# Last block of a streaming encoder step: weight sums behind the pooled frames, pooled products behind za, quarters laid out one by one

## The chip, the cores and the metric

The kernel runs on one core of a Trainium2 chip. The metric is the device time of one execution in microseconds (us). The core has five engines that each work through their own list of instructions in order: TensorE (PE in the profile, with the weight loads as PEld) for matrix products, VectorE (DVE), ScalarE (ACT), GpSimd (POOL) and SyncE (SP). SP does no arithmetic here; its list is a queue of DMA issues. An engine that waits for a semaphore holds everything behind that instruction in its list.

## The reference

One layer of an encoder trunk over 2048 prompt frames and 32 sample frames of width 1024, cut to what the change touches:

```python
hn = rmsnorm(h, g_mix)
hA, bA, cA, zA, vB, zB = split(hn @ w_in)          # six projections of width 512 each
u  = cA * hA
c  = uu[0:T]*conv_w[0] + uu[1:1+T]*conv_w[1] + uu[2:2+T]*conv_w[2] + conv_b   # uu: history, then u
yA = bA * c * silu(zA)
for g, w in enumerate((2, 4, 8, 16)):              # four groups of 128 channels
    pooled_g = trailing_mean(vB_g, w) - vB_g
yB = (pooled @ pool_w) * pool_scale * silu(zB)
h  = h + concat(yA, yB) @ w_out
h  = h + (p @ w_ple) * sigmoid(rmsnorm(h, g_ple) @ w_ple_gate)
y  = rmsnorm(h, g_final)
```

The last two frames of u and the last 15 of vB are returned as well, as states of the streams.

## The kernel before

**Precision.** A product in full float32 accuracy is made of three matmuls on a high and a low part. `split` (L79) makes the parts: ScalarE casts the source to the high part (L80), VectorE subtracts it to get the low part (L81). Nearly every tile that TensorE reads costs one such pair.

**Blocks and units.** The frames are worked in blocks of 448 (288 in the last). Blocks 0 and 1 and blocks 2 and 3 go in pairs; block 4, the last, goes alone. In each of these groups a loop over j = 0..3 makes one `Unit` for 128 channels. This document calls the four units of the last block the first to the fourth; their tiles carry j as a number. A unit of the last block runs `plain`: the products zb, v, c, h, za and b, 24 matmuls of 288 columns each, 12 for each half of the 1024 inputs. Between them come:

- `pool_blocks` after v: VectorE adds up windows of V (win), subtracts (pl), and `split` makes the pooled frames pp. The last block has two segments, 256 prompt frames and 32 sample frames, so all of this is done twice.
- `mix`: three matmuls of pp with the pool weight pw into the bank pm, and a VectorE product into zs.
- U = h * c on VectorE, `conv` on it into c_s (ScalarE's ACTIVATE, then four VectorE instructions), and `states`: four VectorE copies of the ends of U and V into a small tile st.
- `turn_states`: TensorE turns st (pst), ahead of the product b.

**Weights.** The raw columns of w_in come by DMA into the ring `raws` with four slots (raw_zb, raw_v and so on), and are split into w_zb, w_v. The queue on SP issues them in order, each when its slot is free.

**The last block's extra work.** The product with w_out that follows is done in a scheme of seven half-size products, which needs sums of w_out's rows. `early_sums(j)` (L1033) loads two row blocks (wo_r) into two slots of the same ring `raws`, and `weight_sums` makes four differences on VectorE (L180), each with a split: T1 and T3 in place in the first tile, T2 and T4 in the second; their parts are wo_a, wo_b and wo_T. It is called after `u.plain()`. Three of the seven products take whole quarters of w_out instead, 11, 21 and 22, laid out by `layout` (L1298) into wo_c and wo_d with ScalarE's cast (L1303) and VectorE's subtraction (L1304). 11 is laid out first; 21 and 22 after the last frames' parts of the first w_out tile (`rest`, through `tc.issue_after`). The first w_out tile uses 21 in the product y_o and 22 in z_o; in it the steps with weights' high parts come first.

**What sets the order.** The scheduler of the framework orders each engine's list from the dependencies, its own estimates of times and the order in which the code creates instructions. `tc.issue_after(ins)` adds an edge: what the block creates on `ins`'s engine comes behind `ins`.

Of the kernel before, what the change touches and what calls it, by code (L numbers as in the profile page):

```python
# [29 lines left out]
NH = D // 2  # L30
# [7 lines left out]
def trunk(ctx, tc, x_p, x_s, c_conv, c_pool, p_p, p_s, g_mix, w_in, conv_w, conv_b, pool_w,  # L38
# [30 lines left out]
    def rstd_of(ssq, n, name, r=None):  # L69
# [6 lines left out]
        nc.gpsimd.tensor_tensor(r[:n], ms[:n], nhalf[:n], op=ALU.pow)  # L76
        return r

    def split(hi, lo, src, eng=nc.vector):  # L79
        ins = nc.scalar.copy(hi, src)  # L80
        eng.tensor_tensor(lo, src, hi.bitcast(F32), op=ALU.subtract)  # L81
        return ins

    sm = ctx.enter_context(tc.tile_pool(name="sm", bufs=8))
# [259 lines left out]
    with ExitStack() as s1:  # L344
# [187 lines left out]
        def weights(kind, j, name):  # L532

            if first_w:
                return first_w.pop(0)
            raw = raw_weight(kind, j, name)
            out = []
            for half in range(2):
                out.append(wtile(f"w_{name}_{half}"))
                put(out[-1], raw[:, half * KH:half * KH + KH])  # L540
            return out
# [155 lines left out]
        class Unit:  # L697
# [58 lines left out]
            def pool_blocks(self, *bs, late=None):  # L756

                tb, j, V, L = self.tbs[bs[0]], self.j, self.V, self.L
                win = 2 << j
                if self.pooled is None:  # L760
                    self.pw = pool_weight(j)
                    self.pooled = wk.tile([P, 2 * NB], F32R, tag="pp", bufs=1, name=f"pp_{self.tag}")
                    self.rest = {}
                for seg in self.segs(*bs):
                    lo, hi, at, new = seg
                    m = hi - lo
                    v = self.place(V, 15, seg)

                    src, off = V, (L + 15 if new else 0) + 15 + at
                    step, need = 1, win - 2  # L770
                    while step < win:
                        dst = etile(f"win{step}_{self.tag}_{tb}_{new}", 2 * NB + 16)
                        nc.vector.tensor_tensor(dst[:, :m + need], src[:, off - need:off + m],
                                                src[:, off - need - step:off + m - step], op=ALU.add)
                        src, off = dst, need
                        step *= 2
                        need -= step
                    pl = etile(f"pl_{self.tag}_{tb}_{new}", m)
                    skip = 0
                    if tb == 0:  # L780
                        skip = win - 1
                        nc.vector.tensor_tensor(pl[:, :skip], src[:, :skip], cnt[:, first_of(j):first_of(j + 1)],
                                                op=ALU.mult)
                        nc.vector.tensor_tensor(pl[:, :skip], pl[:, :skip], v[:, :skip], op=ALU.subtract)
                    nc.vector.scalar_tensor_tensor(pl[:, skip:], src[:, skip:m], 1.0 / win, v[:, skip:],
                                                   op0=ALU.mult, op1=ALU.subtract)
                    if self.last:

                        self.rest[0] = self.pooled[:, self.n:2 * self.n]
                        lows = self.rest[0][:, lo:hi]  # L790
                    else:
                        lows = etile(f"pq_{self.tag}_{tb}", m, F32R)
                        for i, b in enumerate(bs):
                            self.rest[b] = lows[:, i * self.n:(i + 1) * self.n]
                    parts = self.pooled[:, lo:hi], lows, pl
                    if late is None:
                        split(*parts)
                    else:
                        late.append(parts)

# [11 lines left out]
            def plain(self):  # L812
                tbs, j, tag, zs, V, U, c_s = self.tbs, self.j, self.tag, self.zs, self.V, self.U, self.c_s
                blocks = range(len(tbs))

                def product_of(kind, b, w, between=None):
                    ps = bank(f"{kind}{tag}_{tbs[b]}")
                    project(ps, w, tbs[b], between)
                    return ps[:, :self.n]

                def zb_block(b):
                    nc.scalar.activation(self.cols(zs, b), product_of("zb", b, wz), AF.Silu)

                def v_block(b):
                    ps, o = product_of("v", b, wv), b * self.n
                    for seg in self.segs(b):
                        nc.scalar.copy(self.place(V, 15, seg), ps[:, seg[0] - o:seg[1] - o])
                    self.pool_blocks(b)

                def c_block(b, between=None):  # L830
                    nc.scalar.copy(self.cols(c_s, b), product_of("c", b, wc, between))

                wz, wv = weights("zb", j, f"zb{tag}"), weights("v", j, f"v{tag}")
                if len(tbs) > 1:

                    wc = weights("c", j, f"c{tag}")
                    for b in blocks:
                        zb_block(b)
                        if b:
                            self.mix(b - 1)  # L840
                        v_block(b)
                        if b:
                            next(second)
                            c_block(b)
                        else:
                            for _ in range(3):
                                next(second)
                            vectors()
                            c_block(b, lambda: next(second))
                    self.mix(1)  # L850
                    next(second)
                    self.keep(V, 15, halo_v)
                else:
                    zb_block(0)
                    v_block(0)
                    self.keep(V, 15, halo_v)
                    wc = weights("c", j, f"c{tag}")
                    c_block(0)

                self.history(U, 2, halo_u, hist_u(j))  # L860
                wh = weights("h", j, f"h{tag}")
                for b in blocks:
                    ps = product_of("h", b, wh)
                    for seg in self.segs(b):
                        lo, hi = seg[:2]
                        o = b * self.n
                        nc.vector.tensor_tensor(self.place(U, 2, seg), ps[:, lo - o:hi - o], c_s[:, lo:hi], op=ALU.mult)
                    self.conv(b)
                    if b:
                        next(second)  # L870
                self.keep(U, 2, halo_u)
                if len(tbs) == 1:
                    self.mix(0)
                    st = self.states()
                wza = weights("za", j, f"za{tag}")
                for b in blocks:
                    z = self.cols(V, b)
                    nc.scalar.activation(z, product_of("za", b, wza), AF.Silu)
                    c = self.cols(c_s, b)
                    nc.vector.tensor_tensor(c, c, z, op=ALU.mult)  # L880
                    if b:
                        next(second)
                wb = weights("b", j, f"b{tag}")
                if self.last and j == 3:
                    early_embedding()
                if len(tbs) == 1:
                    self.turn_states(st)
                for b in blocks:
                    ps = product_of("b", b, wb)
                    y = self.cols(c_s, b)  # L890
                    nc.vector.tensor_tensor(y, ps, y, op=ALU.mult)
                    self.store(j, b, c_s)
# [140 lines left out]
        def early_sums(k):  # L1033
            raw = [ring4(raws, f"wo_r{k}_{i}") for i in range(2)]
            for i in range(2):
                nc.sync.dma_start(raw[i], w_out[(i * KH + k) * P:(i * KH + k + 1) * P])
            weight_sums(W, k, *raw)
# [131 lines left out]
        for gi, tbs in enumerate(GROUPS):  # L1169
# [18 lines left out]
            for j in range(4):  # L1188
# [14 lines left out]
                else:  # L1203
                    u.plain()
                if gi == 2:
                    early_sums(j)

        for c in range(EARLY):
            embedding[1](c, c == EARLY - 1)
# [2 lines left out]
    with ExitStack() as s2:  # L1212
# [83 lines left out]
        hold = []  # L1296

        def layout(parts):  # L1298
            for k in range(KH):
                for q, t, c in ("11", tops[k // 2], k % 2), ("21", bots[k], 0), ("22", bots[k], 1):  # L1300
                    if q in parts:
                        hi, src = W[q][0][:, k], t[:, c * NH:c * NH + NH]
                        nc.scalar.copy(hi, src)  # L1303
                        hold.append(nc.vector.tensor_tensor(W[q][1][:, k], src, hi.bitcast(F32), op=ALU.subtract))  # L1304

        quarters("wo", W)
        layout(["11"])
# [398 lines left out]
```

## Time and profile before

| | |
|---|---|
| three runs | 930.24, 931.0 and 933.59 us, median 931.0 |
| profiled execution | 930.78 us, its span 929.0 us |
| last block, first unit's zb to the first w_out product | 454.6 to 553.8 us of the span |
| first w_out tile to the second | 553.8 to 574.3 us |
| mean granted TensorE clock over the span | 0.994 |

The span runs from the first to the last instruction that the profiler recorded; 1.8 us of the time lie around it. Rows of the trace in order of time give the start, the duration, engine, line, operation and tiles, and in brackets how long the engine was idle before the row and what ended that. Rows of busy time by stretch give the stretch, its length, then busy time and number of instructions of PE, PEld, DVE, ACT and POOL, the mean granted clock, the DMA engines' share and GB/s. Rows of waits give the total, how often and the longest. Back-to-back instructions overlap in the records: a VectorE instruction of 512 elements takes 0.69 us, and two take 1.29.

### The profile page before, as it was taken

How to read it: one execution, taken by the hardware profiler on the slowest of the kernel's cores; microseconds unless marked ns; L12 is line 12 of the kernel's file. 1: busy time of each engine (PE TensorE's matmuls, PEld its weight loads, DVE VectorE, ACT ScalarE, POOL GpSimd, SP SyncE). 2: the span in 40 equal slices, each digit the busy share in tenths (PEclk: the TensorE clock that was granted, in tenths of full speed). 3: DMA queues.
4: the chain of work that ended last, by engine and by line, in shares of the span. 5: the costliest groups of instructions: out<-in, count | busy, mean ns of one | idle time of the engine just before them, and what ended most of it. 6: DMA issues, size and time to landing. Idle time of an engine off the chain costs nothing.

```text
span 929.0 us, 12953 instructions
## 1 busy us (share of the span) xinstructions
PE 906.7 (98%) x4485; PEld 791.6 (85%) x4485; DVE 726.0 (78%) x1235; ACT 480.0 (52%) x890; POOL 148.2 (16%) x266
## 2 busy tenths in 40 slices
PE   7999999999999999999979999999999999999996
PEld 5999999999999999999979987888877868888885
DVE  6995998989649888868468888766554699898876
ACT  7743555554434544444345566434424775556455
POOL 4111322401100100000000010111111001233333
PEclk9999999999999999999989999999999999999999
DMA  8354584758974445322867759864784876799793
GB/s 261 98 157 153 165 258 143 216 162 247 396 280 123 140 144 171 80 66 88 290 211 237 224 180 305 266 215 143 241 239 154 291 255 164 189 232 242 198 271 105
DMA packets 141310, 185.91 MB, mean 200 GB/s; under 512 B 12124, under 2 KB 111964, under 8 KB 139965
## 3 DMA queue, kind: packets, MB, share of 16 engines
q1 hardware_dynamic: 120989, 126.53, 44.1%
q0 software_dynamic: 17520, 53.06, 19.8%
q10 hardware_dynamic: 2736, 5.51, 1.8%
q8 instruction: 35, 0.57, 0.3%
q14 instruction: 30, 0.25, 0.1%
HBM read 129.00 MB, written 56.04 MB: 199 GB/s over the span
## 4 chain that ended last, share of the span: by engine, by line
PE 86%; DMA 6%; DVE 5%; ACT 2%; issue 1%; DVEq 0%; ACTq 0%; SPq 0%
PE x_o L170 9%; PE x_g L170 9%; PE x_zbv L577 7%; PE x_ch L577 7%; PE x_zab L577 7%; PE z_g L170 5%; PE z_o L170 4%; PE z_ch L577 4%; PE z_zbv L577 4%; PE z_zab L577 4%; PE e L105 3%; PE y_g L170 2%; PE y_o L170 2%; PE za L577 2%; DMA wo_r<-in_w_out_dram 2%; PE y_ch L577 2%
## 5 line engine op out<-in xcount | busy, mean ns | idle before, releaser
L80 ACT CAST y_S<-y_fS 128x512 fp32r<-128x512 f32 x32 | 19.5, 621 | 40.7 <-PE x_o L170 16.9
L105 PE MATMUL e<-wq,pps 128*128 128x512 f32 (+1 forms) x156 | 38.8, 399 | 0.2 <-ACT pps L80 0.2
L577 PE MATMUL z_zbv<-B,w_zbv_S 128*128 128x448 f32 x168 | 36.7, 367 | 0.0
L577 PE MATMUL z_zab<-B,w_zab_S 128*128 128x448 f32 x168 | 36.7, 367 | 0.0
L577 PE MATMUL x_ch<-B,w_ch_S 128*128 128x448 f32 x168 | 36.6, 367 | 0.0
L577 PE MATMUL z_ch<-B,w_ch_S 128*128 128x448 f32 x168 | 36.6, 366 | 0.0
L577 PE MATMUL x_zab<-B,w_zab_S 128*128 128x448 f32 x168 | 36.5, 366 | 0.0
L577 PE MATMUL x_zbv<-B,w_zbv_S 128*128 128x448 f32 x168 | 36.5, 366 | 0.0
L170 PE MATMUL x_o<-wo_b,y_S 128*128 128x512 f32 x128 | 35.8, 391 | 0.0
L170 PE MATMUL x_g<-wg_b,g_S 128*128 128x512 f32 x128 | 35.7, 389 | 0.0
L577 PEld LDWEIGHTS x_zab<-B,w_zab_S 128*128 128x128 f32 x168 | 31.6, 188 | 2.8
L577 PEld LDWEIGHTS z_ch<-B,w_ch_S 128*128 128x128 f32 x168 | 31.6, 188 | 2.7
L577 PEld LDWEIGHTS x_zbv<-B,w_zbv_S 128*128 128x128 f32 x168 | 31.6, 188 | 2.7
L577 PEld LDWEIGHTS z_zab<-B,w_zab_S 128*128 128x128 f32 x168 | 31.5, 188 | 2.8
L577 PEld LDWEIGHTS x_ch<-B,w_ch_S 128*128 128x128 f32 x168 | 31.5, 188 | 2.7
L577 PEld LDWEIGHTS z_zbv<-B,w_zbv_S 128*128 128x128 f32 x168 | 31.4, 188 | 2.6
L1433 POOL DMA_DIRECT2D e<-h_d x28 | 24.8, 907 | 53.8 <-DVE e L1430 43.3
L105 PEld LDWEIGHTS e<-wq,pps 128*128 128x128 f32 (+1 forms) x156 | 27.4, 182 | 6.9 <-ACT pps L80 0.5
L72 POOL TENSOR_SCALAR ms_x<-ssq_x 128x1 f32<-128x1 f32 (+1 forms) x17 | 12.5, 738 | 117.3 <-ACT junk L91 117.0
L80 ACT CAST y<-y 128x512 fp32r<-128x512 f32 x24 | 14.8, 619 | 29.6 <-PE x_o L170 14.1
L80 ACT CAST g_S<-g_fS 128x512 fp32r<-128x512 f32 x32 | 19.0, 618 | 19.2 <-DVE g_fS L1609 13.2
L170 PEld LDWEIGHTS x_o<-wo_b,y_S 128*128 128x128 f32 x128 | 23.9, 188 | 5.2 <-ACT c_o L1236 0.3
(601 smaller groups left out, 2621.7 us busy)
## 6 DMA issues: line engine op xcount, KB each, us to landing
y<-y_d SPq DMA_DIRECT2D x16, 512.0 KB, 6.1
x<-in_x_prompt_dram SPq DMA_DIRECT2D x16, 512.0 KB, 5.6
h_d<-x SPq DMA_DIRECT2D x16, 512.0 KB, 2.8
hn<-h_d SPq DMA_DIRECT2D x61, 128.0 KB, 6.6
e<-e_d SPq DMA_DIRECT2D x15, 512.0 KB, 6.2
xt<-in_x_prompt_dram SPq DMA_DIRECT2D x14, 512.0 KB, 6.5
e<-h_d POOLq DMA_DIRECT2D x28, 256.0 KB, 6.9
out_dram<-e POOLq DMA_DIRECT2D x13, 512.0 KB, 4.2
```

What stands on the lines that cost most here:

```text
L72: nc.gpsimd.tensor_scalar(ms[:n], ssq[:n], scalar1=1.0 / D, scalar2=EPS, op0=ALU.mult, op1=ALU.add)
L80: ins = nc.scalar.copy(hi, src)
L105: nc.tensor.matmul(ps[:n], pps[:, a, k, :n], wp[k][b][:, cs], start=k + q == 0, stop=k == 1 and q == 2)
L170: nc.tensor.matmul(ps[:n], lhs[:, k, a, :n], w[b][:, k], start=start and k + q == 0, stop=k == KH - 1 and q == 2, skip_group_check=True)
L577: nc.tensor.matmul(ps[:, :b.shape[-1]], lhs[:, k, x], b[:, k, y], start=start and k + q == 0, stop=stop and k == KH - 1 and q == 2, skip_g ...
L1433: nc.gpsimd.dma_start(ee, h_d[r:r + P, at[1] * NH:at[1] * NH + NH], accum_op=ALU.add)
```

## The change

Three edits, all in the last block and the first w_out tile:

1. The ScalarE cast and the VectorE subtraction of the last `split` of a unit's pooled frames are kept (`self.behind`), and everything that `early_sums` puts on these two engines comes behind them.
2. `mix(0)` of a unit of the last block is created after the product za and what follows it, no longer between h and za.
3. `layout` goes through one quarter after the other, no longer through row blocks with the quarters inside.

No instruction is added or taken away. In the code:

```diff
+    ends = []
+
     def split(hi, lo, src, eng=nc.vector):
         ins = nc.scalar.copy(hi, src)
-        eng.tensor_tensor(lo, src, hi.bitcast(F32), op=ALU.subtract)
+        ends[:] = ins, eng.tensor_tensor(lo, src, hi.bitcast(F32), op=ALU.subtract)
         return ins
...
                     if late is None:
                         split(*parts)
+                        self.behind = tuple(ends)
...
                 if len(tbs) == 1:
-                    self.mix(0)
                     st = self.states()
                 wza = weights("za", j, f"za{tag}")
                 for b in blocks:
...
                     if b:
                         next(second)
+                if len(tbs) == 1:
+                    self.mix(0)
                 wb = weights("b", j, f"b{tag}")
...
                 if gi == 2:
-                    early_sums(j)
+                    with tc.issue_after(u.behind[0].ins), tc.issue_after(u.behind[1].ins):
+                        early_sums(j)
...
         def layout(parts):
-            for k in range(KH):
-                for q, t, c in ("11", tops[k // 2], k % 2), ("21", bots[k], 0), ("22", bots[k], 1):
-                    if q in parts:
-                        hi, src = W[q][0][:, k], t[:, c * NH:c * NH + NH]
-                        nc.scalar.copy(hi, src)
-                        hold.append(nc.vector.tensor_tensor(W[q][1][:, k], src, hi.bitcast(F32), op=ALU.subtract))
+            for q in parts:
+                for k in range(KH):
+                    t, c = {"11": (tops[k // 2], k % 2), "21": (bots[k], 0), "22": (bots[k], 1)}[q]
+                    hi, src = W[q][0][:, k], t[:, c * NH:c * NH + NH]
+                    nc.scalar.copy(hi, src)
+                    hold.append(nc.vector.tensor_tensor(W[q][1][:, k], src, hi.bitcast(F32), op=ALU.subtract))
```

The lines of the changed kernel stand two to five further down (L81 is L83 there, L1303 is L1308).

What this does to the order, first on VectorE in the first unit. Before, the first row sum stood ahead of the window additions, and the pooled frames came between sums:

```order
L180 TENSOR_TENSOR wo_r_0_4474<-wo_r_0_4474 128x512
L773 TENSOR_TENSOR win_2_0_4_0_4296<-V_0_4216 128x256
L81 TENSOR_TENSOR w_b_0_0_4433<-raw_b_0_4431,w_b_0_0_4433 128x4x128
L785 SCALAR_TENSOR_TENSOR pl_0_4_0_4298<-win_2_0_4_0_4296,V_0_4216 128x256
L81 TENSOR_TENSOR w_b_0_1_4436<-raw_b_0_4431,w_b_0_1_4436 128x4x128
L81 TENSOR_TENSOR pp_0_4295<-pl_0_4_0_4298,pp_0_4295 128x256
L773 TENSOR_TENSOR win_2_0_4_1_4302<-V_0_4216 128x32
L81 TENSOR_TENSOR wo_a<-wo_r_0_4474,wo_a 128x512
L785 SCALAR_TENSOR_TENSOR pl_0_4_1_4304<-win_2_0_4_1_4302,V_0_4216 128x32
L180 TENSOR_TENSOR wo_r_0_4474<-wo_r_1_4475,wo_r_0_4474 128x512
L81 TENSOR_TENSOR pp_0_4295<-pl_0_4_1_4304,pp_0_4295 128x32
```

Now the last low part of pp stands ahead of the sums; from there to U and the second copy of U into st, the rows are:

```order
L83 TENSOR_TENSOR pp_0_4295<-pl_0_4_1_4304,pp_0_4295 128x32
L182 TENSOR_TENSOR wo_r_0_4474<-wo_r_0_4474 128x512
L182 TENSOR_TENSOR wo_r_0_4474<-wo_r_1_4475,wo_r_0_4474 128x512
L83 TENSOR_TENSOR w_zb_1_0_4498<-raw_zb_1_4496,w_zb_1_0_4498 128x4x128
L83 TENSOR_TENSOR wo_a<-wo_r_0_4474,wo_a 128x512
L83 TENSOR_TENSOR wo_b<-wo_r_0_4474,wo_b 128x512
L870 TENSOR_TENSOR U_0_4217<-h_0_4_4352,c_s_0_4218 128x256
L870 TENSOR_TENSOR U_0_4217<-h_0_4_4352,c_s_0_4218 128x32
L1019 COPY st_0_4385<-U_0_4217 128x2
L182 TENSOR_TENSOR wo_r_1_4475<-wo_r_1_4475,wo_r_0_4474 128x512
L811 SCALAR_TENSOR_TENSOR c_s_0_4218<-U_0_4217,vec,c_s_0_4218 128x256
```

The pooled frames have left the sums behind them, while U stays behind sums and behind the first low part of the next unit's w_zb, as it was; the second copy of U into st follows after c_s's four instructions.

On TensorE in the first unit, before:

```order
L577 MATMUL h_0_4_4352<-hn_4192,w_h_0_1_4349 128x288 x12
L749 MATMUL pm_0_0_4385<-pp_0_4295,pw_4290 128x288
L750 MATMUL pm_0_0_4385<-pp_0_4295,pw_4290 128x288
L751 MATMUL pm_0_0_4385<-pp_0_4295,pw_4290 128x288
L577 MATMUL za_0_4_4404<-hn_4192,w_za_0_0_4398 128x288 x12
L577 MATMUL za_0_4_4404<-hn_4192,w_za_0_1_4401 128x288 x12
L1024 MATMUL pst_0_4439<-ident,st_0_4391 34x128
```

and now:

```order
L579 MATMUL h_0_4_4352<-hn_4192,w_h_0_1_4349 128x288 x12
L579 MATMUL za_0_4_4398<-hn_4192,w_za_0_0_4392 128x288 x12
L579 MATMUL za_0_4_4398<-hn_4192,w_za_0_1_4395 128x288 x12
L751 MATMUL pm_0_0_4425<-pp_0_4295,pw_4290 128x288
L752 MATMUL pm_0_0_4425<-pp_0_4295,pw_4290 128x288
L753 MATMUL pm_0_0_4425<-pp_0_4295,pw_4290 128x288
L1028 MATMUL pst_0_4439<-ident,st_0_4385 34x128
```

The 24 matmuls of za stand ahead of pm, and pst follows pm at once. The second unit is changed in the same way; in the third and fourth pm stood among za's matmuls and now stands behind them.

On ScalarE in the first w_out tile, the casts of quarters 21 (into wo_c) and 22 (into wo_d), before:

```order
L1303 CAST wo_c<-wo_q_5448 128x512
L1303 CAST wo_d_5459<-wo_q_5448 128x512
L1303 CAST wo_c<-wo_q_5449 128x512
L1303 CAST wo_d_5459<-wo_q_5449 128x512
L1303 CAST wo_c<-wo_q_5450 128x512
L1303 CAST wo_d_5459<-wo_q_5450 128x512
L1303 CAST wo_c<-wo_q_5451 128x512
L1303 CAST wo_d_5459<-wo_q_5451 128x512
```

and now:

```order
L1308 CAST wo_c<-wo_q_5448 128x512
L1308 CAST wo_c<-wo_q_5449 128x512
L1308 CAST wo_c<-wo_q_5450 128x512
L1308 CAST wo_c<-wo_q_5451 128x512
L1308 CAST wo_d_5459<-wo_q_5448 128x512
L1308 CAST wo_d_5459<-wo_q_5449 128x512
L1308 CAST wo_d_5459<-wo_q_5450 128x512
L1308 CAST wo_d_5459<-wo_q_5451 128x512
```

All four of 21 now come ahead of the four of 22; VectorE's low parts move in the same way.

## The prediction

> **What bounds the kernel now.** I read the page first, then TensorE's waits, then the stretch in which they lie. On the page TensorE is the engine without slack.
>
> ```profile
> span 929.0 us, 12953 instructions
> PE 906.7 (98%) x4485; PEld 791.6 (85%) x4485; DVE 726.0 (78%) x1235; ACT 480.0 (52%) x890; POOL 148.2 (16%) x266
> ```
>
> Of the 22.3 us in which it does no matmul, the view of waits puts 8.5 us into the stretch from 454 to 575 us, where the last block and the first w_out product lie. It names the two things the change touches: pm (pooled products) behind ACT's cast of pp (pooled frames), and y_o behind ACT's cast of wo_c (quarter 21).
>
> ```profile
> PE pm L749 <- ACT pp L80: 8.0, 4, 5.4
> PE y_o L165 <- ACT wo_c L1303: 0.5, 1, 0.5
> ```
>
> The view of busy time by stretch shows the four units (three of them from zb to zb), then the first w_out product and the second. The column behind POOL's is the granted TensorE clock. In the second product TensorE has no free time, so a gain before it stays a gain to the end, unless a transfer holds it.
>
> ```profile
> 467.40:482.20 14.80, 9.36 (x54) 9.07 (x54) 12.84 (x35) 8.80 (x19) 2.04 (x4) 0.77 0.53 155
> 482.20:502.60 20.40, 20.08 (x150) 19.59 (x149) 17.04 (x45) 12.01 (x27) 1.62 (x4) 1.00 0.70 211
> 502.60:523.70 21.10, 19.89 (x150) 19.63 (x149) 18.20 (x49) 11.90 (x27) 2.38 (x5) 1.00 0.73 218
> 523.70:545.20 21.50, 20.46 (x155) 20.17 (x154) 17.95 (x46) 10.96 (x24) 0.92 (x2) 1.00 0.66 208
> 553.80:574.30 20.50, 19.94 (x86) 15.67 (x86) 17.04 (x28) 11.02 (x21) 1.98 (x3) 1.00 1.04 318
> 574.30:593.60 19.30, 19.30 (x86) 15.60 (x85) 16.91 (x28) 9.31 (x17) 3.13 (x6) 1.00 0.79 257
> ```
>
> TensorE's order in time gives the beat (zb, v, c, h, za, b are a unit's projections, pst turns its state st):
>
> ```profile
> 464.15 3.33 PE L577 MATMUL h<-hn,w_h 128*128 128x288 f32 x24
> 472.93 0.61 PE L749 MATMUL pm<-pp,pw 128*128 128x288 f32 x1 [5.44 <-ACT pp L80]
> 478.90 0.27 PE L1024 MATMUL pst<-ident,st 128*34 128x128 f32 x1
> 482.18 3.34 PE L577 MATMUL zb<-hn,w_zb 128*128 128x288 f32 x24
> 485.35 3.33 PE L577 MATMUL v<-hn,w_v 128*128 128x288 f32 x24
> 502.64 3.34 PE L577 MATMUL zb<-hn,w_zb 128*128 128x288 f32 x24
> 523.74 3.34 PE L577 MATMUL zb<-hn,w_zb 128*128 128x288 f32 x24
> 541.32 0.60 PE L133 MATMUL ptp<-ident,ep 128*128 128x128 f32 x4
> ```
>
> From zb to v are 3.17 us, the full pace of 24 matmuls: 0.13 each. The wait before pm also costs clock:
>
> ```profile
> 469.50:470.50 1.00, 0.00 (x0) 0.00 (x0) 1.00 (x4) 0.88 (x2) 0.00 (x0) 1.00 0.27 68
> 470.50:471.50 1.00, 0.00 (x0) 0.00 (x0) 1.00 (x4) 0.86 (x3) 0.00 (x0) 0.70 0.06 15
> 477.50:478.00 0.50, 0.50 (x5) 0.50 (x4) 0.50 (x4) 0.26 (x1) 0.00 (x0) 0.77 0.87 245
> ```
>
> A mean of 0.70 is full speed for 0.4 us and half after it, so the clock fell at 470.9; by the 0.77 it came back at 477.7. Half of the 4.8 us from 472.93 to 477.7 is 2.4 us lost. The first unit thus stalls for 5.4 + 2.4 = 7.8 us.
>
> **The first unit, sums pinned and pm behind za.** VectorE and ScalarE, and the queue that feeds them:
>
> ```profile
> 463.70 0.38 SPq L527 DMA_DIRECT2D raw_zb<-in_w_in_dram  x1
> 468.89 0.69 DVE L180 TENSOR_TENSOR wo_r<-wo_r 128x512 f32<-128x512 f32 x1 [7.26 <-DMA wo_r<-in_w_out_dram]
> 471.88 0.62 ACT L80 CAST w_zb<-raw_zb 128x512 fp32r<-128x512 f32 x1 [0.28 <-DMA raw_zb<-in_w_in_dram]
> 475.20 0.51 DVE L867 TENSOR_TENSOR U<-h,c_s 128x256 f32<-128x256 f32 x2
> 476.06 0.91 ACT L806 ACTIVATE c_s<-U,vec 128x256 f32<-128x256 f32 x2
> 477.81 0.16 DVE L1016 COPY st<-U 128x2 f32<-128x2 f32 x1
> ```
>
> Before, the first sum stands ahead of the window additions and waits 7.26 us for its rows; the pooled frames come after it. Put ahead of the sum they no longer wait for those rows, and the page names nothing else that they waited for. So pp is ready before h ends, at 464.15 + 3.17 = 467.3. No wait stands ahead of za now: it ends at 470.5, and pm's three matmuls at 470.9.
>
> Next on TensorE is pst, ahead of b, and here the wait comes back. pst needs both copies of U into st, U comes behind h on VectorE, and ahead of U stand the sums and the low part of w_zb, which needs raw_zb. That load is issued at 463.70 with nothing changed ahead of it in its queue, and lands at 471.88 again. From there: ScalarE casts w_zb, wo_a, w_zb, wo_b at 0.52 us apart (pace from the wo_c rows below), so wo_b's cast starts at 471.88 + 3 x 0.52 = 473.4 and ends at 474.1. VectorE's low part of wo_b takes 0.6, and U starts at 474.7, half a us earlier than before, not 7. From U to the second st copy were 2.61 us, with the 0.43 us of zs in between, which is now later; I take 2.3. pst then starts at 474.7 + 2.3 + 0.16 = 477.15. TensorE waits 470.9 to 477.15: 6.2 us where it was 5.4.
>
> What is gained is that za lies ahead of the wait; what is lost is that b comes out of it at half clock. At the old 2.4 us of clock loss b ends at 477.15 + 0.03 + 3.28 (pst to zb before) + 2.4 = 482.9, against 482.18: **0.7 us later**. Without any clock loss it would be 1.7 us earlier, and with a cold stretch of 6.8 us, twice the 3.4 between matmuls' end and the fall, 1.7 later; these are the ends, and I take the row's 2.4. [...]
>
> **The other three units.** A unit at full pace is 6 x 3.17 for its projections, 0.4 for pm, 0.15 for pst: 19.6 us. From zb to zb were 20.46 and 21.10, so 0.85 and 1.5 go. The fourth, zb to ptp, was 17.58 against 5 x 3.17 + 0.4 = 16.25: 1.3. That is 3.65; I take 3.55, since the small matmuls' change of weights costs something. Each wait was under 3.4 us and the clock stayed at 1.00.
>
> The same st stands behind the same chain here, so its time must be bounded:
>
> ```profile
> 484.19 1.14 ACT L80 CAST w_h<-raw_h 128x512 fp32r<-128x512 f32 x2 [2.78 <-DMA raw_h<-in_w_in_dram]
> 484.85 1.29 DVE L81 TENSOR_TENSOR w_h<-raw_h,w_h 128x512 fp32r<-128x512 f32 x2 [0.66 <-ACT w_h L80]
> 488.94 0.38 SPq L527 DMA_DIRECT2D raw_zb<-in_w_in_dram  x1
> 491.70 3.34 PE L577 MATMUL h<-hn,w_h 128*128 128x288 f32 x24
> 494.03 1.14 ACT L80 CAST w_zb<-raw_zb 128x512 fp32r<-128x512 f32 x2 [0.77 <-DMA raw_zb<-in_w_in_dram]
> 510.02 0.38 SPq L527 DMA_DIRECT2D raw_zb<-in_w_in_dram  x1
> 514.72 1.14 ACT L80 CAST w_zb<-raw_zb 128x512 fp32r<-128x512 f32 x2 [0.74 <-DMA raw_zb<-in_w_in_dram]
> ```
>
> With raw_zb at 494.0: cast 0.62, low parts of w_zb and wo_a 1.2, U 0.43, low part of wo_b 0.6, copy: st at 497.2. TensorE wants it at 482.9 + 5 x 3.17 + 0.4 = 499.1; 1.9 us to spare. In the third, 514.72 leads to 517.7, wanted at 518.7: 1.0 us. Pinned sums also hold their two slots of the raw ring longer, so raw_c and raw_h of the next unit are issued later, behind the last sum. raw_h moved by a us still leaves w_h at 487.1 where TensorE wants it at 491.7. Nothing is priced for it, and cover ends at some 4 us. y_d<-zs falls behind zs (it moves with pm, some 3 us later) in SP's queue, ahead of raw_h: same cover. POOL's queue is unchanged. In the fourth unit the sums fall into the e products, where their first use is 11 us away; the cover there is VectorE, busy 17.95 of 21.5.
>
> **The quarters one by one.**
>
> ```profile
> 562.80 0.62 ACT L1303 CAST wo_c<-wo_q 128x512 fp32r<-128x512 f32 x1
> 564.91 1.14 PE L165 MATMUL y_o<-wo_c,y 128*128 128x512 f32 x3
> 565.93 0.61 ACT L1303 CAST wo_c<-wo_q 128x512 fp32r<-128x512 f32 x1
> 566.59 1.45 PE L165 MATMUL y_o<-wo_c,y 128*128 128x512 f32 x5 [0.54 <-ACT wo_c L1303]
> 567.75 0.68 DVE L1304 TENSOR_TENSOR wo_d<-wo_q,wo_d 128x512 fp32r<-128x512 f32 x1
> 568.80 2.89 PE L165 MATMUL z_o<-wo_d,y_S 128*128 128x512 f32 x12
> ```
>
> The casts go 21, 22, 21, ...: the fourth of 21 is the seventh, 6 x 0.52 behind the first. y_o's fourth matmul could start at 564.91 + 3 x 0.24 (2.89 over 12) = 565.6 and starts at 566.59: 1.0 us. In the new order the fourth 21 starts at 564.4 and ends at 565.0. The wait goes: **1.0 us**. Next late would be 22, whose last cast ends at 567.1 as before, while z_o then starts at 567.8; 0.7 us to spare. The low parts end at 568.4, wanted eight matmuls into z_o.
>
> **Sum** on the profiled execution: 930.78 + 0.7 - 3.55 - 1.0 = 926.9 us. Its own time is 0.2 below the median of the three runs (931.0), within their spread, so I leave it there: 0.44% faster, just inside the 0.5% (4.7 us) that a measurement of this kernel can tell from no change.
>
> **Rivals.**
> - *The first unit's wait goes altogether*, as pm's wait being named 5.4 suggests: 930.78 - 7.8 - 4.55 = 918.4. For it: pp is ready early. Against it: U behind w_zb. 0.05.
> - *The wait stays, the clock does not fall*, or returns sooner: b ends 1.7 us early, 930.78 - 1.7 - 4.55 = 924.5. [...] 0.15.
> - *st is late in the second and third unit too.* raw_zb took 8.2 us from issue to cast in the first, 5.1 and 4.7 in these. At 8.2 again TensorE would wait 1.2 and 2.5 us: 930.6, no change. [...] For it: in-order VectorE and thin slack. Against it: the queue in front is the same. Slower 0.09, no change 0.06.
> - *The gain is eaten on the way*: VectorE's sums beside the e products make y or wo_c late for the first product, by 1 to 2 us: 928.5. 0.15.
>
> **How the numbers follow.** The sum itself 0.50. Of it, at a scatter of 1 to 1.5 us, 0.22 ends below 926.3 and so beyond 0.5%, 0.28 above. Faster: 0.05 + 0.15 + 0.22 = 0.42; same: 0.28 + 0.06 + 0.15 = 0.49; slower 0.09. The range leaves out the first rival and most of the slower case: 923.5 (the cold stretch missing, and a us more) to 931.5 (st late at 8.2 us, and a us more). The likeliest's own range is 925.5 to 928.5.
>
> **What will show it.** TensorE's waits from 454 to 575 should name pst, behind VectorE's st, with some 6 us once, no pm and no y_o. The granted clock should be 0.5 in b of the first unit and 1.00 in za. From zb to zb 19.6 twice. U at 474.7 behind w_zb. It is wrong if U starts near 468 (then the first rival), if pst waits in more than one unit, or if the two w_out products no longer take 19.3 to 20.5 us.

## The result and the profile after

Over 22 runs each, before took 931.89 us (median, 929.79 to 934.08) and the changed kernel 928.62 us (926.26 to 931.61): a ratio of 0.9966, 95% interval 0.9956 to 0.9976. That is 0.34% faster: the interval leaves out 1, and the gain is within the 0.5% bound of the prediction, whose time was 926.9 us and whose range was 923.5 to 931.5.

The profiled execution of the changed kernel was its slowest, 931.61 us, span 929.8 us. It is read by stretches, not by its end. TensorE's waits between 440 and 580 us:

```profile
PE pst L1028 <- DVE st L1020: 6.9, 1, 6.9
PE ptp L135 <- DVE zs L755: 0.7, 1, 0.7
PE pm L751 <- ACT pp L82: 0.3, 1, 0.3
PE pm L752 <- DVE pp L83: 0.3, 1, 0.3
```

pm's 8.0 us and y_o's 0.5 have become one wait of pst and three small ones. TensorE's order in time:

```profile
466.92 3.34 PE L579 MATMUL h<-hn,w_h 128*128 128x288 f32 x24
470.10 3.34 PE L579 MATMUL za<-hn,w_za 128*128 128x288 f32 x24
473.27 0.30 PE L751 MATMUL pm<-pp,pw 128*128 128x288 f32 x1
480.73 0.40 PE L1028 MATMUL pst<-ident,st 128*34 128x128 f32 x1 [6.89 <-DVE st L1020]
486.37 3.37 PE L579 MATMUL zb<-hn,w_zb 128*128 128x288 f32 x24
505.98 3.34 PE L579 MATMUL zb<-hn,w_zb 128*128 128x288 f32 x24
525.56 3.34 PE L579 MATMUL zb<-hn,w_zb 128*128 128x288 f32 x24
567.35 1.98 PE L167 MATMUL y_o<-wo_c,y 128*128 128x512 f32 x8
```

The reader is to see that pm follows za at once, that three zb stand 19.6 us apart, and that y_o is one unbroken row of eight. The granted clock (the column behind POOL's) fell during pst's wait and came back near the end of b:

```profile
474.00:476.00 2.00, 0.00 (x0) 0.00 (x0) 0.43 (x1) 0.58 (x2) 0.00 (x0) 0.94 0.18 44
476.00:478.00 2.00, 0.00 (x0) 0.00 (x0) 1.66 (x3) 2.00 (x5) 0.00 (x0) 0.50 0.02 5
484.00:486.00 2.00, 2.00 (x11) 2.00 (x10) 1.22 (x3) 0.62 (x1) 0.40 (x1) 0.50 0.73 188
486.00:488.00 2.00, 2.00 (x17) 2.00 (x16) 1.43 (x4) 0.62 (x1) 0.00 (x0) 1.00 1.09 301
```

The stretches of this and of every later kernel, read from the starts of rows in TensorE's order (us; the first column runs from h of the first unit to zb of the second, the next two from zb to zb, the fourth from zb to the first e product, the last from the first w_out tile to the second). Ratios are to the kernel before, with their intervals:

| kernel | ratio | first unit | second | third | fourth | w_out tile |
|---|---|---|---|---|---|---|
| before | 1 | 18.03 | 20.46 | 21.10 | 21.51 | 20.50 |
| all three edits | 0.9966 (0.9956 to 0.9976) | 19.45 | 19.61 | 19.58 | 22.15 | 19.43 |
| pins | 0.9976 (0.9961 to 0.9991) | 18.41 | 19.63 | 20.93 | 21.81 | 20.47 |
| mix | 1.0009 (0.9994 to 1.0025) | 18.84 | 19.56 | 23.89 | 21.10 | 20.46 |
| layout | 0.9991 (0.9973 to 1.0009) | 18.00 | 20.82 | 20.67 | 21.60 | 19.41 |
| store | 0.9965 (0.9949 to 0.998) | 18.31 | 19.61 | 19.58 | 21.14 | 19.38 |
| store_mix3 | 0.9966 (0.9949 to 0.9983) | 18.02 | 19.58 | 19.58 | 21.39 | 19.46 |
| u_first | 0.9965 (0.9947 to 0.9984) | 10.06 | 26.47 | 20.65 | 21.49 | 19.44 |
| loads | 0.9906 (0.9879 to 0.9934) | 10.06 | 19.56 | 21.24 | 21.42 | 19.43 |
| u_first_loads | 0.9939 (0.9922 to 0.9957) | 10.06 | 22.73 | 22.28 | 21.51 | 19.50 |
| loads_before | 1.0 (0.9984 to 1.0016) | 14.40 | 21.90 | 23.77 | 21.16 | 20.41 |
| best | 0.9874 (0.9855 to 0.9893) | 10.06 | 20.56 | 20.36 | 22.31 | 19.39 |

The profiled execution reached h of the first unit at 466.92 us against 464.15 before, though nothing ahead of it was changed. The granted clock was at half early in this execution, where the profile of before has 1.00:

```profile
16.00:19.00 3.00, 3.00 (x13) 2.78 (x13) 3.00 (x7) 1.64 (x4) 0.00 (x0) 0.50 1.12 351
```

From there on it ran late: the first 12 matmuls of a product c began at 31.98 us, against 28.78 before. The other kernels share that stretch too, and they reached h at 463.4 to 465.0, so these 2.8 us belong to the execution.

### The profile page after: what moved, and what is told of

Same layout as the page of the kernel before. It is cut to its first block, busy times and chain, and to the rows that moved or that the text cites. A ratio compares the mean times of both kernels' runs of the same rounds, so it can differ in the third digit from the quotient of the medians.

```text
span 929.8 us, 12958 instructions
## 1 busy us (share of the span) xinstructions
PE 906.7 (98%) x4485; PEld 793.5 (85%) x4485; DVE 727.4 (78%) x1235; ACT 479.7 (52%) x890; POOL 146.2 (16%) x266
## 3 DMA queue, kind: packets, MB, share of 16 engines
q0 software_dynamic: 17520, 53.06, 19.6%
## 4 chain that ended last, share of the span: by engine, by line
PE 87%; DVE 6%; DMA 3%; issue 2%; ACT 1%; SPq 0%; POOL 0%; ACTq 0%; DVEq 0%
PE x_o L172 9%; PE x_g L172 9%; PE x_zab L579 7%; PE x_zbv L579 7%; PE x_ch L579 7%; PE z_g L172 5%; PE z_o L172 4%; PE e L107 4%; PE z_zab L579 4%; PE z_zbv L579 4%; PE z_ch L579 4%; PE y_g L172 2%; PE y_o L172 2%; PE b L579 2%; PE y_zab L579 2%; PE y_zbv L579 2%
## 5 line engine op out<-in xcount | busy, mean ns | idle before, releaser
L579 PE MATMUL x_zab<-B,w_zab_S 128*128 128x448 f32 x168 | 36.5, 366 | 0.0
L579 PE MATMUL x_ch<-B,w_ch_S 128*128 128x448 f32 x168 | 36.5, 366 | 0.0
L579 PE MATMUL x_zbv<-B,w_zbv_S 128*128 128x448 f32 x168 | 36.5, 366 | 0.0
L579 PE MATMUL z_ch<-B,w_ch_S 128*128 128x448 f32 x168 | 36.5, 366 | 0.0
L1236 DVE TENSOR_TENSOR c_o<-x_o,x 128x512 f32<-128x512 f32 x14 | 9.7, 690 | 23.9 <-PE x_o L172 23.9
```

The lines of the kernel that those rows point to most:

```text
L579: nc.tensor.matmul(ps[:, :b.shape[-1]], lhs[:, k, x], b[:, k, y], start=start and k + q == 0, stop=stop and k == KH - 1 and q == 2, skip_g ...
L1236: add = lambda o, a, b: nc.vector.tensor_tensor(o, a, b, op=ALU.add)
```

## The experiments

**One edit at a time.** `pins` has the first edit alone, `mix` the second, `layout` the third:

```diff
# pins
+                    with tc.issue_after(u.behind[0].ins), tc.issue_after(u.behind[1].ins):
+                        early_sums(j)
# mix
-                    self.mix(0)            # between h and za
+                    self.mix(0)            # behind za
# layout
-            for k in range(KH):
-                for q, t, c in ...
+            for q in parts:
+                for k in range(KH):
```

> The first edit alone (sums behind the pooled frames; mix and layout as before). Theory: pp is ready early, so pm no longer waits in any unit; in the first unit the wait comes back in front of pst behind st, some 6 us once, with the cold clock in b, and h to the next zb is 19 to 20 us (18.0 before). Second and third unit 19.6 us each (20.46 and 21.10 before). The load of the fourth unit's raw_za stands ahead of the store y_d<-c_s in SP's list here, so the fourth unit keeps its gain: zb to e 20.2 to 20.8 us (21.51 before, 22.15 with all edits). Sum against before: +1.4 - 2.4 - 1.0 = -2.0 us, ratio 0.998. Rival (the pins alone do nothing, what counts is that pm stands behind za): pm named with waits as before, ratio 1.000.

> The second edit alone (pm behind za; sums stand among the pooled frames as before). Theory: in the second and third unit the old wait for pp was 0.85 and 1.5 us, less than za's 3.17, so it goes here too: 19.6 us each. In the first unit pm's wait was 5.4, less 3.17: pm and then pst still wait until st is there, pst starts about where it did against h (14.75 us after h's start), and the cold clock lies in b: h to zb 19 to 20 us. Fourth unit: raw_za ahead of the store y_d<-c_s in SP's list, gain kept: zb to e 20.2 to 20.8. Sum about -2 us, ratio 0.998, like the pins alone: the two edits take the same waits. Rival (the pins are what counts, the late pooled frames hold zs and the stores): units at 20.4 and more, ratio 1.000.

> The third edit alone (quarters laid out one by one). Theory: y_o's wait for quarter 21 goes, first w_out tile to the second 19.4 to 19.5 us instead of 20.50, nothing else moves: -1.0 us, ratio 0.9989. Rival: the gain is given back in the second tile or to quarter 22 (z_o waits): ratio 1.000.

TensorE's waits (440 to 600 us) of `pins`, then of `mix`:

```profile
PE pst L1027 <- DVE st L1019: 6.2, 1, 6.2
PE pm L751 <- ACT pp L82: 1.8, 2, 1.0
PE y_o L167 <- ACT wo_c L1307: 0.5, 1, 0.5
```

```profile
PE pm L749 <- ACT pp L80: 5.0, 2, 2.6
PE pst L1025 <- DVE st L1017: 4.0, 1, 4.0
PE ptp L133 <- DVE zs L753: 0.5, 1, 0.5
```

`pins` moved the first unit's wait to pst, as expected, and cleaned the second unit, but the third still waits 1.0 us for pp and the fourth 0.8. The pins take the sums out of pp's way, yet pp's last columns come too late for a pm right behind h. In the third unit their cast starts 13.6 us behind zb, and h ends at 12.7. With all edits it starts at 11.7, so the second edit did not only put za in front of pm: pp itself comes earlier there, with raw_za issued 0.2 us behind zb instead of 1.5. The fourth unit took 21.81 us, not the 20.2 to 20.8 expected, and in `mix` 21.10. `mix` took the same waits only in part: with the sums still among the pooled frames, pp of the third unit came 2.4 us later than pm wanted it even behind za, and this cost clock as well:

```profile
521.63 0.40 PE L749 MATMUL pm<-pp,pw 128*128 128x288 f32 x1 [2.43 <-ACT pp L80]
```

```profile
522.00:523.00 1.00, 1.00 (x9) 0.96 (x9) 1.00 (x4) 1.00 (x4) 0.00 (x0) 1.00 0.00 0
523.00:524.00 1.00, 1.00 (x7) 1.00 (x6) 1.00 (x4) 1.00 (x4) 0.00 (x0) 0.52 0.22 55
526.00:527.00 1.00, 1.00 (x8) 1.00 (x7) 1.00 (x5) 0.41 (x1) 0.46 (x1) 0.77 0.50 146
```

So my expectation that each edit takes the same waits alone was wrong: they need each other in the third unit. `layout` did in the trace what was expected, 19.41 us for the tile and y_o without a wait; in time, 0.9991, it is not told apart from nothing.

**The fourth unit.** With all edits it is 0.6 us slower than before. SP's queue and ScalarE's cast of w_za there, before:

```profile
523.53 0.37 SPq L527 DMA_DIRECT2D raw_za<-in_w_in_dram  x1
525.10 0.34 SPq L741 DMA_DIRECT2D y_d<-c_s  x1
...
528.81 1.14 ACT L80 CAST w_za<-raw_za 128x512 fp32r<-128x512 f32 x2 [0.28 <-DMA raw_za<-in_w_in_dram]
```

and after:

```profile
527.32 0.34 SPq L743 DMA_DIRECT2D y_d<-c_s  x1
527.71 0.43 SPq L529 DMA_DIRECT2D raw_za<-in_w_in_dram  x1
...
533.62 1.14 ACT L82 CAST w_za<-raw_za 128x512 fp32r<-128x512 f32 x2 [1.65 <-DMA raw_za<-in_w_in_dram]
```

The store, which needs the third unit's b, now stands ahead of the load. Against the unit's zb (523.74 and 525.56) the load went from 0.2 us ahead to 2.15 behind, and the cast from 5.1 us behind to 8.1. TensorE itself does not miss these weights: their low parts are done at 535.56, and za starts at 538.25. But VectorE's list has the window additions behind them, so pp comes late:

```profile
534.27 1.29 DVE L83 TENSOR_TENSOR w_za<-raw_za,w_za 128x512 fp32r<-128x512 f32 x2 [1.58 <-ACT w_za L82]
535.48 0.43 DVE L775 TENSOR_TENSOR win<-V 128x270 f32<-128x270 f32 x1
```

The windows start 9.9 us behind zb, 7.0 before. The store is not the whole cause. In `pins` the load still stands ahead of it, and is just as late against that unit's zb (523.96):

```profile
526.03 0.39 SPq L529 DMA_DIRECT2D raw_za<-in_w_in_dram  x1
527.00 0.39 SPq L743 DMA_DIRECT2D y_d<-c_s  x1
```

There the loads ahead of it are late, because the pinned sums hold their slots of the ring longer: raw_c is issued 0.8 us ahead of zb, raw_h 1.5 behind; before they were 5.0 and 0.8 ahead, with all edits 1.95 ahead and 0.8 behind. For a row sum SP waits 6.7 us ahead of raw_c with all edits, 4.6 before. `store` moves the store to another queue; `store_mix3` also creates the fourth unit's pm ahead of za again:

```diff
-                nc.sync.dma_start(y_d[chunk, ...], self.cols(t, b))
+                (nc.gpsimd if self.last and chunk == 2 else nc.sync).dma_start(y_d[chunk, ...], self.cols(t, b))
# store_mix3, besides
+                    if j == 3:
+                        self.mix(0)
```

> All three edits, and the third unit's store y_d<-c_s goes to GpSimd's queue, so that SP's list has the load of raw_za directly behind raw_h. Theory (the fourth unit lost its gain because that load stands behind the store): raw_za is issued some 2 us earlier, w_za's low part no longer holds the window additions, zb to e of the fourth unit 20.2 to 20.5 us instead of 22.15, no wait of pm and of ptp for zs: -1.7 to -1.9 us against all three edits, ratio to before 0.9946 to 0.9950. Rival (VectorE's sums beside the fourth unit's work are the cause): zb to e stays at 22.15, ratio 0.9966 as with all three edits.

> All three edits, the store y_d<-c_s of the third unit on GpSimd's queue, and pm of the fourth unit created ahead of za again (the scheduler puts it among za's matmuls). Theory (the other half of the fourth unit's lost gain is ptp, which waits 0.7 us for zs, because zs comes only after pm and pm now stands right ahead of ptp): ptp has no wait, zb to e 20.2 to 20.5 us instead of 21.14, ratio to before 0.9955 to 0.996. Rival (pp of the fourth unit is late again, pm waits among za): pm waits about 1 us, zb to e stays at 21.1, ratio 0.9965.

The fourth unit of `store`:

```profile
537.17 0.29 PE L751 MATMUL pm<-pp,pw 128*128 128x288 f32 x1
...
537.63 0.38 PE L135 MATMUL ptp<-ident,ep 128*128 128x128 f32 x2
...
539.91 0.44 PE L135 MATMUL ptp<-ident,ep 128*128 128x128 f32 x2 [0.72 <-DVE zs L755]
```

From zb (521.31) to ptp are 16.32 us, where all edits had 17.35, and the unit takes 21.14 instead of 22.15: 1.0 us of the expected 1.7 to 1.9, in one execution each. In time this can't be seen (0.9965 against 0.9966). raw_za was still issued 1.4 us behind zb, since raw_c and raw_h are as late as with all edits, and the windows start 8.6 us behind zb. What TensorE still waits for is zs, ahead of ptp: pm now stands right ahead of it, and zs reads pm's bank. `store_mix3` took that wait away, but pm waited 0.7 us for pp instead, and the unit took 21.39. Here the rival was right: with the pooled frames this late on VectorE, TensorE waits at one place or the other.

**The first unit: order or landing.** `u_first` puts U, the conv and st ahead of the sums and of the second unit's w_zb on VectorE and ScalarE. `loads` leaves those pins as they are and issues the loads for the first w_out tile behind raw_v of the second unit. `u_first_loads` does both, `loads_before` moves the loads in the kernel before the change:

```diff
# u_first
+                    if j == 0:
+                        u.behind = u.conv_end, u.turned
# and, for the second unit's weights,
+                        s3.enter_context(tc.issue_after(last_unit[0].turned.ins))
+                        s3.enter_context(tc.issue_after(last_unit[0].conv_end.ins))
# loads
-                first_y = load_y(0, 2 * P)
-                first_x = load_rows(ya, "x", 0, x_p)
-                tops = [ring4(ya, f"wo_q{i}") for i in range(2)]
-                for k in range(KH):
-                    load_top(k, tops[k // 2])
...
+                if unit == 9:
+                    with tc.issue_after(issued["v2_1"].ins):
+                        first_y = load_y(0, 2 * P)
+                        ...
```

> All three edits, and in the first unit U, the conv and both copies of U into st go ahead of the first row sum and of the second unit's w_zb on VectorE and ScalarE (pins on the conv's last ACTIVATE and on the second copy; the loads stay as they are). Theory (pst waits only because U stands behind the low part of w_zb, and so behind raw_zb's landing): U starts about 3.4 us after h's start instead of 11.3, pst has no wait, b runs at full clock. The second unit's zb then waits for its own weights: raw_zb lands 7.6 to 8.5 us after h's start, so zb starts 10 to 13 us after h instead of 19.45 (18.3 in the run with the store moved). The second unit can give back some of it, because raw_c is issued only when the sums free the ring. Together -4 to -8 us against all three edits, ratio to before 0.988 to 0.992. Rival (the loads are the bound, whatever the order): the wait only moves on to zb, c or h of the second unit, ratio 0.9966 as with all three edits.

> All three edits, and the loads that the first w_out tile needs (y, x and four row blocks of w_out, 2.5 MB) are issued behind raw_v of the second unit instead of ahead of wo_r and raw_zb. Theory (raw_zb lands late because the DMA engines are full with these): raw_zb is issued 2 to 4 us earlier against h's start and has up to 2.5 MB less in front of it, some 6 us at 390 GB/s; it lands 4 to 6 us earlier, U follows it, pst waits 1 to 3 us instead of 6 to 6.9, and the clock may stay: h to the second unit's zb 12 to 15 us instead of 18.3 to 19.5, ratio to before 0.990 to 0.992. The fourth unit keeps its late raw_za (22.15). Rival (what holds U is the chain of sums, not the landing, or hn and the other loads fill the queue anyway): pst waits 5 us or more, ratio 0.9966.

> Both at once: U ahead of the sums and of w_zb, and the loads for the first w_out tile behind raw_v. If landing and order are two halves of one wait, U first takes pst's wait away and the earlier landing takes the wait of the second unit's zb away: h to zb 10.1 to 11 us (full pace), ratio to before 0.986 to 0.989. If the ring of four slots is the bound (raw_c issued behind the sums), the second unit takes 22 us or more instead of 19.6 and the sum is no better than the better one of the two.

> The kernel before the change, with only the loads for the first w_out tile issued behind raw_v of the second unit. Theory (the first unit's wait of 5.4 us is the landing of wo_r and raw_zb and not the place of the sums): with the rows landing 4 to 6 us earlier pm waits under 1.5 us in the first unit and the clock stays; h to zb 10.5 to 12 us instead of 18.03. The waits of the other units (0.31, 1.21 and 1.04 us) and y_o's 0.54 stay. Ratio to before 0.991 to 0.993, and the three edits are then worth 0.2 to 0.3% on top of it. Rival (sums ahead of the pooled frames hold pm however early the rows land): pm waits 4 us or more in some unit, ratio 0.997 or more.

With `u_first` pst had no wait in the first unit, and zb of the second waited instead, and then ran at half clock (0.50 granted from 479 to 485 us):

```profile
479.43 5.65 PE L579 MATMUL zb<-hn,w_zb 128*128 128x288 f32 x22 [3.95 <-DVE w_zb L83]
```

First and second unit together took 36.5 us instead of 39.1, the third lost 1.1 of that again, and the ratio, 0.9965, is that of all edits. The wait moved on, as the rival had it, but this run does not show that the landing alone holds zb. ScalarE cast the first half of w_zb as soon as it had landed, while the low parts came 6.7 us later:

```profile
471.96 0.62 ACT L82 CAST w_zb<-raw_zb 128x512 fp32r<-128x512 f32 x1 [2.43 <-DMA raw_zb<-in_w_in_dram]
478.69 1.29 DVE L83 TENSOR_TENSOR w_zb<-raw_zb,w_zb 128x512 fp32r<-128x512 f32 x2
```

Between them VectorE did two of the sums and the low parts of all four, which this order puts ahead of w_zb. With `loads`, raw_zb and U in the first unit, and what TensorE still waits for:

```profile
461.79 0.38 SPq L531 DMA_DIRECT2D raw_zb<-in_w_in_dram  x1
...
465.61 0.62 ACT L82 CAST w_zb<-raw_zb 128x512 fp32r<-128x512 f32 x1 [0.49 <-DMA raw_zb<-in_w_in_dram]
...
468.68 0.52 DVE L872 TENSOR_TENSOR U<-h,c_s 128x256 f32<-128x256 f32 x2
```

```profile
PE pst L1030 <- DVE st L1022: 1.2, 1, 1.2
PE ptp L135 <- DVE zs L757: 0.7, 1, 0.7
```

With all edits these stood at:

```profile
467.14 0.38 SPq L529 DMA_DIRECT2D raw_zb<-in_w_in_dram  x1
475.42 0.62 ACT L82 CAST w_zb<-raw_zb 128x512 fp32r<-128x512 f32 x1 [7.66 <-DMA raw_zb<-in_w_in_dram]
478.24 0.52 DVE L870 TENSOR_TENSOR U<-h,c_s 128x256 f32<-128x256 f32 x2
```

From issue to cast raw_zb took 3.8 us instead of 8.3, and against h (464.29) it was issued 2.7 us earlier. The first row sum, which with all edits waited 4.4 us for its rows, waited for none. The whole first stall is gone, clock included (b's 24 matmuls took 3.45 us, with all edits 5.76): 10.06 us instead of 19.45, better than the 12 to 15 expected. The median of six runs is 923.03 us, 0.9906. The profiled execution was their fastest, 919.81; where the others, up to 925.97, lost more was not seen. `u_first_loads` has 0.9939; its interval overlaps that of `loads`, but its four units take 4.3 us more in the trace. With the early landing too, w_zb's low part stands behind all four sums (475.11, its cast 468.52), and zb waited 1.3 us for it; pst waited 1.4 us in the second unit and 1.5 in the third for st, whose copies stand among the sums. `loads_before` shows the surprise: nothing gained.

```profile
PE pm L751 <- ACT pp L80: 7.2, 4, 2.4
PE y_o L165 <- ACT wo_c L1308: 0.5, 1, 0.5
```

The first unit did gain 3.6 us, but the second and third lost 1.4 and 2.7. In these two the first sum now stands ahead of the window additions and waits there for its rows, 1.37 and 2.34 us. pm waited 2.2, 1.9, 2.4 and 0.7 us, and the first and third of these cost clock (0.50 granted from 472 to 475 and from 517 to 519 us). So the earlier landing shortens the first stall with either order, and the whole of it goes, with nothing lost behind it in the second unit, only where the order keeps the sums off pp: loads alone 1.000, edits alone 0.9966, both 0.9906.

**Both repairs together.** `best` is `loads` with the store on GpSimd's queue and the copies of U into st created ahead of the conv.

```diff
+                    if len(tbs) == 1:
+                        st = self.states()
                     self.conv(b)
...
-                if len(tbs) == 1:
-                    st = self.states()
```

> The moved loads, with two repairs: the third unit's store y_d<-c_s goes to GpSimd's queue, and the copies of U into st are created ahead of the conv, so that in the third unit the second copy no longer comes behind c_s's four VectorE instructions (with the moved loads alone pst waited 1.19 us there). Theory: first unit h to zb 10.1 us, second and third unit 19.6 us each, fourth 20.4 to 21.2 us (21.42 with the moved loads alone); 1.5 to 2.5 us less than the moved loads alone, ratio to before 0.988 to 0.989. Rival (VectorE has no slack left, each wait taken away appears in the next unit): ratio 0.990 to 0.991, as with the moved loads alone.

Its median is 921.54 us over five runs, 0.9874, the fastest of all and a little past the 0.988 to 0.989 expected. But its interval overlaps that of `loads`, so the two repairs are not shown to be worth anything. Its trace speaks for the rival: against `loads` the third unit gained 0.9 us, while the second and fourth lost 1.0 and 0.9, as one wait went and others came, all for VectorE:

```profile
PE pst L1030 <- DVE st L1022: 1.1, 2, 0.8
PE ptp L135 <- DVE zs L757: 0.7, 1, 0.7
PE zb L581 <- DVE w_zb L83: 0.4, 1, 0.4
PE pm L754 <- DVE pp L83: 0.3, 1, 0.3
```

## Why the prediction was right, and where it was not

- *The first unit, 0.7 us later.* Right in mechanism: pm's wait came back at pst behind U and raw_zb, 6.9 us for 6.2, and b ran at half clock (0.50 granted from 481 to 485 us). This execution was 1.4 us later. `store` and `store_mix3` have the same first unit and took 18.31 and 18.02; the mean of the three is 18.6 against 18.03 and 18.00 (`layout`) with the old order, so 0.6 later. U came 11.3 us after h's start here and 10.5 and 10.3 in those two; the prediction had 10.55. The difference is raw_zb's: ScalarE cast it 8.5 us after h's start here, where the prediction took 7.7.
- *Second and third unit, 0.85 and 1.5 us.* Measured 0.85 and 1.52. The slack of st, put at 1.9 and 1.0 us, was 1.6 and 1.0:

```profile
500.92 0.16 DVE L1020 COPY st<-U 128x2 f32<-128x2 f32 x1
...
521.07 0.16 DVE L1020 COPY st<-U 128x2 f32<-128x2 f32 x1
```

  pst started at 502.68 and 522.25. The rival with st late did not happen; with `loads`, where the second copy came behind c_s's four instructions in the third unit, it did, at 1.2 us.
- *The fourth unit, 1.3 us: this step failed.* It took 0.64 us more instead of 1.3 less, an error of 1.9. The sum named the loads that come later but priced nothing for them, because it counted their cover up to TensorE's use of the weights. There it did hold; what it does not cover is VectorE's list, in which the windows come behind w_h's and w_za's low parts. It named raw_h and y_d<-zs as what moves in SP's queue. It did not look at y_d<-c_s, which now stands ahead of raw_za, and took the cover of raw_h for the cover of all. `store` puts 1.0 us of the 1.9 there; what the late raw_c and raw_h cost by themselves no run shows. It also counted pm's move as pure gain, though pm arrived right in front of ptp, which waits 0.7 us for zs. `store_mix3` shows that this second part was not to be had: pp itself was late.
- *The quarters, 1.0 us.* Measured 1.07, and 1.09 alone; z_o had no wait.
- *The sum.* Predicted was 3.85 us less. The five stretches of the two profiles give +1.42 - 0.85 - 1.52 + 0.64 - 1.07 = -1.4, and -2.2 with the first unit's mean of 0.6; from the second tile to the end 354.15 instead of 354.75 us, another 0.6. The medians say 3.3, interval 2.2 to 4.1. That this lies near 3.85 is luck in part: the stretches that were priced give 2.2, and no edit touches the one that gives 0.6. The sum stood on an execution of 930.78 us, 1.1 below the later median of before; that is most of the 1.7 us between 926.9 and 928.62.
- *The rivals.* The wait that goes altogether (918.4) needed the loads moved: `loads` had it in its profiled execution. The clock that does not fall was not seen in any profile with a wait of 5.2 us or more; its 0.15, and the 0.09 for a slower kernel, were the author's estimates. "Eaten on the way" gave 928.5, the nearest number, by another mechanism: e to the first w_out product took 8.51 us as before (8.50); what was lost went one stage earlier, in the fourth unit.

## What to carry to other kernels

When a wait ends with a DMA's landing, moving the waiting instruction may only move the wait, as here from pm to pst and then to zb; ask also what stands in front of that load, and issue what is needed much later behind it. A cover counted for one moved load says nothing of those behind it in the same queue: follow each of them to its first user, on every engine, and look at what stands behind that user in the engine's list. And try a move of loads and a move of the work that uses them together, since one of them alone can be worth nothing.

## What the runs showed of the hardware

- Waits of 2.20 to 2.43 us cost clock too. In `mix` TensorE was idle for 2.43 us up to 521.63; the clock stayed at 1.00 until 523.04 (0.52 as a mean of 523 to 524), 1.4 us after work had begun again, and was back at 526.5 (0.77 as a mean of 526 to 527), so half of 3.4 us was lost. Waits of 2.20 and 2.41 us in `loads_before` cost the same way (0.50 from 472 to 475 and from 517 to 519 us); waits of 1.89 there and of 1.21 before did not (1.00 behind both). In the kernel before, the clock fell at 470.9, after 3.4 us without a matmul (467.5 to 470.9); the shorter waits show that so long an idle stretch was not needed. The prediction's "each wait was under 3.4 us and the clock stayed" held for its rows and is no rule; what decides that the clock falls was not shown. Behind the waits of 5.2 to 6.9 us the clock was low (0.50) for 6.8 us in five profiles and for 10.2 us in that of all edits.
- With 2.5 MB for a later stage issued in front, a load of 0.5 MB took 8.3 us from issue to use (raw_zb with all edits, 467.14 to 475.42), 3.8 without (`loads`, 461.79 to 465.61); with all edits, from 476 to 478 us, in the wait behind it, the DMA engines carried 5 GB/s.
- In two of the twelve profiles, those of all edits and of `pins`, the clock fell already near 15 us (0.82 and 0.81 as means of 13 to 16 us, 1.00 in the other ten), in a stretch that all the kernels share.
